# A mixer's output gates: six at the end and ten in the branch phase, or all sixteen between the stages of its heads

## The chip, the cores and the metric

The kernel runs on one core of a Trainium2 chip. The metric is the device time of one execution in microseconds (us): before the change 2744.16 us, the median of three runs (2744.15 to 2745.08).

## What is computed

The reference runs three residual blocks over 512 tokens of width 1024: twice a mixer and a gated convolutional feed-forward layer (`DEPTH = 2`), then a second kind of block with four mixers and an MLP. The change touches the mixer of the first two. Cut to what matters:

```
p = h @ w_in                                  # h: 512 x 1024, normalised
qkv, z, beta_r, a_r, hq, hf_fwd, hf_bwd, hi, hgate, gate_dn, gate_hg = split(p)
# four heads of a gated delta rule, forward and backward in time
o_dn = gated_rmsnorm(delta(q, k, v, beta, g) + flip(delta(flip(...))), z, dn_norm)
# four heads of HGRN2, forward and backward
o_hg = gated_rmsnorm(hgrn2(...) + flip(hgrn2(flip(...))), hgate, hg_norm)
merged = sigmoid(gate_dn) * (o_dn @ w_branch_dn) + sigmoid(gate_hg) * (o_hg @ w_branch_hg)
x = x + merged @ w_out
```

`gate_dn` and `gate_hg` are 1024 wide each: the sixteen output gates are the sixteen column blocks of 128 of the two. They depend on `h` alone, not on any head.

## The kernel before

Activations lie transposed, 128 features on the partitions by 512 tokens. A matrix product is a `gemm` (L264) of one block of 128 output columns: `weights` (L236) loads the weight block `wr` by a DMA of the SP queue (three buffers), ACT casts it to `wh` (L245) and DVE makes the remainder `wl` (L246), two buffers each; then three matmuls for each of the eight blocks of 128 input features (`xh wh`, `xl wh`, `xh wl`, L257 through `mm`) add up in one of two PSUM banks `pd`. So a gate is 24 matmuls, an `evac` on DVE (L394) that multiplies by the norm `rb`, and a sigmoid on ACT (L746). A branch product has four input blocks and is 12 matmuls.

`mixer` (L719) has two phases. In the **head phase** the string `ORDER` (L171) sets the stages: for each of four heads a `gdn_front` (f: three gemms, a convolution), a `gdn_inverse` (i: six levels in which PE, DVE and ACT wait for each other, L528 to L540), an `hg_head` (h: four gemms, then seven levels over the tile `pq`, L680 to L690) and a `gdn_scan` (s: four steps, each a chain of `pp`, `r`, `pw`, `w`, `pu`, `S2`, L580 to L603). Scan and `hg_head` end in `head_out` (L616): a gemm, the square of the output (L623), its sum over the partitions by a matmul with ones (L299), Ln and Exp (L294, L295), a product on POOL (L626) and one on DVE (L628). The scan loads its decays `er` by a DMA of the ACT queue (L566), takes their exponential on ACT (L567) and multiplies on POOL (L569). Each engine works its own list in order; a scheduler that lays the instructions out on a modelled timeline makes the lists, stages that come earlier in `ORDER` ahead, inverses and scans raised in priority, so that gemms of later stages stand between the links of their chains.

After the heads come six gates whose matmuls are **paced**: `mm` queues them behind marked steps of the last scan, eight after each mark (`PACE`, L259). In the **branch phase** the outputs are split into `xh` and `xl` (L286, L287); for each of eight m come a product with `w_bh` (evacuated at L764), one with `w_bd` (L768), a sum on POOL (L769), a split, and two further gates, ten in all, computed when they are next needed. Six buffers `g` hold the gates. Then `w_out`.

## Time and profile before

| | |
|---|---|
| median of three runs | 2744.16 us |
| span of the profiled execution, first to last instruction | 2742.3 us |
| median less this span | 1.9 us |
| PE busy, share of the span | 2645.3 us, 96% |
| DVE, ACT, POOL busy | 57%, 41%, 12% |
| mean granted TensorE clock | 0.983 of 2.4 GHz |

The profile is of one execution; the pages and stretches below count from its first instruction. Head phase and last scan lie at about 0 to 440 us in the first mixer and 950 to 1390 in the second, the branch phases at 440 to 540 and 1390 to 1495. PE's busy time counts matmuls whose pipelines overlap: one of 512 columns is shown with 0.39 us but the next starts 0.23 us after it, so a busy PE isn't always at its pace, and the number of matmuls in a stretch says more than its busy time. PEclk is the granted clock; 0.5 is 1.2 GHz.

### The profile page before, as it was taken

Reading aid. Unit: us, or ns where it says so; the run is one execution under the profiler, and the core shown is the slowest. Engines: PE = TensorE matmul, PEld = TensorE weight load, DVE = VectorE, ACT = ScalarE, POOL = GpSimd, SP = SyncE. Lnnn points to the kernel's source line nnn. Section 1 sums busy time; section 2 is a strip of 40 time slices with the busy share of each in tenths; the row PEclk is TensorE's granted clock in tenths of the full one; section 3 lists DMA queues with packets and bytes.
Section 4 is the critical chain, followed back from the end, with each engine's and each line's share of the span. In section 5 each row is a group of like instructions: output and inputs, shape, how many; then the busy total and the mean of one; then the engine's idle time right before and its main releaser. Section 6 shows DMA issues by size and latency. Waiting matters only on the chain.

```text
span 2742.3 us, 32455 instructions
## 1 busy us (share of the span) xinstructions
PE 2645.3 (96%) x12674; PEld 2178.6 (79%) x12674; DVE 1556.6 (57%) x2234; ACT 1124.7 (41%) x1511; POOL 329.2 (12%) x282
## 2 busy tenths in 40 slices
PE   7999899999999979998999999999999999999999
PEld 4788788878888857887888788888777788888887
DVE  6778764455554366778644555534874444553442
ACT  6545544343333255455443433333446443332221
POOL 1112320001110011122200011100100111000000
PEclk9999989999999999999999999999999999999999
DMA  4112212253223332111123423234411232433332
GB/s 149 62 49 67 62 39 68 88 167 100 94 98 114 121 89 70 55 61 54 39 76 101 160 95 100 93 121 127 145 64 51 82 96 94 140 129 99 94 104 88
DMA packets 99064, 254.13 MB, mean 93 GB/s; under 512 B 10016, under 2 KB 31520, under 8 KB 98656
## 3 DMA queue, kind: packets, MB, share of 16 engines
q1 hardware_dynamic: 66960, 215.17, 24.5%
q10 hardware_dynamic: 31568, 35.85, 4.5%
q8 instruction: 100, 1.64, 0.2%
q0 software_dynamic: 384, 1.05, 0.1%
q14 instruction: 52, 0.43, 0.1%
HBM read 238.36 MB, written 12.62 MB: 92 GB/s over the span
## 4 chain that ended last, share of the span: by engine, by line
PE 49%; ACT 1%; DVE 0%; issue 0%; POOL 0%; ACTq 0%; DVEq 0%; POOLq 0%
PE pd L257 45%; PE ph L1065 1%; PE pl L1053 1%; PE pd L259 1%; ACT wh L245 0%; PE pr L1061 0%; ACT L1179 0%; PE pl L972 0%; PE ph L682 0%; PE pl L843 0%; DVE wl L246 0%; ACT rb L294 0%; ACT rb L295 0%; PE pl L1015 0%; PE ph L1039 0%
## 5 line engine op out<-in xcount | busy, mean ns | idle before, releaser
L257 PE MATMUL pd<-xh,wh 128*128 128x512 f32 (+1 forms) x3186 | 1265.8, 398 | 36.3 <-DVE raw L449 14.3
L257 PE MATMUL pd<-xh,wl 128*128 128x512 f32 (+1 forms) x3188 | 1258.0, 395 | 2.6 <-DVE wl L246 2.3
L257 PE MATMUL pd<-xl,wh 128*128 128x512 f32 (+1 forms) x3186 | 1253.7, 394 | 2.1 <-DVE xl L290 2.0
L245 ACT ACTIVATE wh<-wr 128x1024 fp32r<-128x1024 f32 (+5 forms) x449 | 434.9, 969 | 1011.3 <-PE pd L257 866.8
L257 PEld LDWEIGHTS pd<-xh,wh 128*128 128x128 f32 (+1 forms) x3186 | 600.2, 188 | 178.8 <-issue 20.9
L257 PEld LDWEIGHTS pd<-xl,wh 128*128 128x128 f32 (+1 forms) x3186 | 600.3, 188 | 139.2 <-issue 7.2
L257 PEld LDWEIGHTS pd<-xh,wl 128*128 128x128 f32 (+1 forms) x3188 | 600.0, 188 | 138.7 <-DVE wl L246 5.0
L246 DVE TENSOR_TENSOR wl<-wr,wh 128x1024 fp32r<-128x1024 f32 (+5 forms) x449 | 521.7, 1162 | 250.3 <-ACT wh L245 244.1
L1179 ACT ACT_TABLE_LOAD x116 | 148.8, 1283 | 8.7 <-issue 4.4
L394 DVE TENSOR_TENSOR g<-pd,rb 128x512 f32<-128x512 f32 x64 | 44.3, 692 | 158.2 <-PE pd L257 148.1
L803 POOL TENSOR_TENSOR fs<-fs,rb 128x512 f32<-128x512 f32 x44 | 56.9, 1294 | 506.3 <-ACT fs L802 506.3
L682 PE MATMUL ph<-pq,kc 128*128 128x128 f32 x448 | 74.8, 313 | 19.6 <-POOL er L569 6.7
L797 DVE TENSOR_TENSOR fg<-pd,rb 128x512 f32<-128x512 f32 x44 | 30.5, 693 | 109.9 <-PE pd L257 107.0
L682 PEld LDWEIGHTS ph<-pq,kc 128*128 128x128 f32 x448 | 66.7, 213 | 26.4 <-issue 19.2
L687 POOL TENSOR_TENSOR pq<-pq,f 128x512 f32<-128x512 f32 x48 | 58.8, 1225 | 230.7 <-PE ph L682 211.5
L805 DVE TENSOR_TENSOR fs<-fs,pd 128x512 f32<-128x512 f32 x44 | 30.3, 688 | 90.0 <-POOL fs L803 90.0
L801 DVE SCALAR_TENSOR_TENSOR fs<-fg,cv,fs 128x512 f32<-128x512 f32 x88 | 65.9, 749 | 3.6 <-ACT fs L799 1.9
L802 ACT ACTIVATE fs<-fs 128x512 f32<-128x512 f32 x44 | 27.8, 632 | 85.5 <-DVE fs L801 85.5
L394 DVE TENSOR_TENSOR mh<-pd,rb 128x512 f32<-128x512 f32 x32 | 22.1, 692 | 70.2 <-PE pd L257 68.8
L680 ACT COPY kc<-qk 128x512 f32<-128x512 f32 x56 | 36.9, 659 | 52.2 <-PE ph L682 44.5
L454 DVE SCALAR_TENSOR_TENSOR qk<-raw,cv,qk 128x512 f32<-128x512 f32 x64 | 54.1, 858 | 2.6 <-ACT qk L452 2.2
L684 DVE COPY_PREDICATED att<-um,ph 128x512 f32<-128x512 uint8 x56 | 41.2, 736 | 21.5 <-PE ph L682 21.2
(332 smaller groups left out, 2442.5 us busy)
## 6 DMA issues: line engine op xcount, KB each, us to landing
wr<-in_w_in_dram SPq DMA_DIRECT2D x126, 512.0 KB, 3.3
wr<-in_w_up_dram SPq DMA_DIRECT2D x88, 512.0 KB, 3.3
wr<-in_w_m_dram SPq DMA_DIRECT2D x64, 512.0 KB, 3.8
wr<-in_w_dn_dram SPq DMA_DIRECT2D x32, 512.0 KB, 3.6
wr<-in_w_gt_dram SPq DMA_DIRECT2D x32, 512.0 KB, 3.3
wr<-in_w_out_dram SPq DMA_DIRECT2D x24, 512.0 KB, 3.4
xd<-xn ACTq DMA_DIRECT2D x40, 256.0 KB, 2.0
xo<-xd ACTq DMA_DIRECT2D x32, 256.0 KB, 2.8
```

The source lines that it names most:

```text
L245: nc.scalar.activation(hi, raw, AF.Copy)
L246: (nc.vector if lo == "v" else nc.gpsimd).tensor_tensor(lw, raw, hi.bitcast(F32), op=ALU.subtract)
L257: return self.nc.tensor.matmul(*a, **k)
L394: self.nc.vector.tensor_tensor(out, ps, rb, op=ALU.mult)
L454: V.scalar_tensor_tensor(o, raw[:, j:j + T], self.col(f"dnc{l}_{j}", ch), o, op0=ALU.mult, op1=ALU.add)
L680: A.copy(kc.rearrange("p (n e b) -> p n e b", e=2, b=hh), self.pair(qk, T, hh, 0, 0, T))
L682: PE.matmul(pl[:, c], kc[:, c * P:(c + 1) * P], self.pair(pq, T, hh, 1, c * P, P), start=True, stop=True)
L684: V.copy_predicated(att, self.um[:, o:o + P].unsqueeze(1).to_broadcast([P, 4, P]), pl)
L687: (G if hh > 1 else V).tensor_tensor(halves(pq, hh, True), halves(pq, hh, True), tot(F, n, 0, n + 1, hh), op=ALU.mult)
L801: nc.vector.scalar_tensor_tensor(g, gp[:, j:j + T], self.col(f"fc{l}_{j}", m), g, op0=ALU.mult, op1=ALU.add)
L803: nc.gpsimd.tensor_tensor(g, g, rb, op=ALU.mult)
L1179: nc.scalar.preload_act_table_set(s)
```

## The change

The six gates after the heads and the ten of the branch phase go. `ORDER` gets ten times `g1` and a last `g6`: all sixteen gates are computed in the head phase, as stages of their own. The first ten are stored unscaled to DRAM (`gs`, SP queue) and come back in the branch phase into tiles `gl` of their own (SP queue); the last six stay in the `g` buffers. All sixteen sigmoids are taken at the branch phase's start. `issue_after`, the marks and `PACE` are gone. Docstrings, which are gone as well, are left out here.

```
-NP = 6
-PACE = 8
-ORDER = "f0 i0 f1 h0 s0 i1 f2 h1 s1 i2 f3 h2 s2 i3 h3 s3"
+KEEP = 6
+NL = 10
+ORDER = "f0 i0 f1 g1 h0 g1 s0 g1 i1 f2 g1 h1 g1 s1 g1 i2 f3 g1 h2 g1 s2 g1 i3 h3 g1 s3 g6"
...
     def mm(self, *a, **k):
-        if not self.pace:
-            return self.nc.tensor.matmul(*a, **k)
-        with self.tc.issue_after(self.pace[0]):
-            self.nc.tensor.matmul(*a, **k)
-        self.paced += 1
-        if self.paced % PACE == 0:
-            self.pace.pop(0)
+        return self.nc.tensor.matmul(*a, **k)
...
+                def gate():
+                    i = len(gates)
+                    s = self.evac(self.gemm([W[(GD0, GH0)[i % 2] + i // 2]], xs), rb, gt, "g", NG)
+                    if i < 2 * KD - KEEP:
+                        t = self.dr.tile([P, T], F32, name=self.nmx("gs"), tag=f"gs{i}")
+                        nc.sync.dma_start(t, s)
+                        s = t
+                    gates.append(s)
...
+                    if u[0] == "g":
+                        for _ in range(h):
+                            gate()
...
-                for i in range(NG - NP):
-                    gate(i)
-                self.pace = self.marks[:]
-                for i in range(NG - NP, NG):
-                    gate(i)
-                self.pace = []
...
+                for i in range(2 * KD):
+                    t = gates[i] if i >= 2 * KD - KEEP else mg.tile([P, T], F32, name=self.nmx("gl"), tag="gl", bufs=NL)
+                    if i < 2 * KD - KEEP:
+                        nc.sync.dma_start(t, gates[i])
+                    nc.scalar.activation(t, t, AF.Sigmoid)
+                    gates[i] = t
...
-                        for i in range(2 * m - 2 + NG, min(2 * m + NG, 2 * KD)):
-                            gate(i)
```

What it does to the engines' lists is seen at three places of the first mixer. Numbers behind a name tell tiles apart; the changed kernel's lines are some ten lower (L254 is L257 here, L669 is L682, L520, L527 and L530 are L528, L535 and L538, L291 is L299, L278 is L286).

**PE, the last head's inverse and `hg_head`** (`pl` banks are the inverse's levels, `ph` the levels of `hg_head`). Before:

```order
L528 MATMUL pl_552_2869<-zt_529_2773,br_527_2769 128x128 x4
L682 MATMUL ph_599_3117<-pq_570_2939,kc_600_3118 128x128 x4
L535 MATMUL pl_554_2876<-v_553_2874,zc_555_2877 128x128 x4
L538 MATMUL pl_556_2883<-zc_555_2877,v_553_2874 128x128 x4
L682 MATMUL ph_601_3128<-pq_570_2939,kc_602_3129 128x128 x4
L528 MATMUL pl_557_2890<-zt_529_2773,br_527_2769 128x128 x4
L682 MATMUL ph_603_3139<-pq_570_2939,kc_604_3140 128x128 x4
L535 MATMUL pl_559_2897<-v_558_2895,zc_560_2898 128x128 x4
L538 MATMUL pl_561_2904<-zc_560_2898,v_558_2895 128x128 x4
L682 MATMUL ph_605_3150<-pq_570_2939,kc_606_3151 128x128 x4
L545 MATMUL pl_564_2913<-zt_529_2773,bn_526_2767 128x128 x4
L682 MATMUL ph_607_3161<-pq_570_2939,kc_608_3162 128x128 x4
```

In the changed list, at the same place:

```order
L254 MATMUL pd_716_3728<-xh_10_111,wh_718_3730 128x512
L254 MATMUL pd_716_3728<-xl_11_112,wh_718_3730 128x512
L254 MATMUL pd_716_3728<-xh_10_111,wl_719_3731 128x512
L669 MATMUL ph_649_3410<-pq_624_3254,kc_650_3411 128x128 x4
L254 MATMUL pd_716_3728<-xh_12_116,wh_718_3730 128x512
L254 MATMUL pd_716_3728<-xl_13_117,wh_718_3730 128x512
L254 MATMUL pd_716_3728<-xh_12_116,wl_719_3731 128x512
L254 MATMUL pd_716_3728<-xh_15_123,wh_718_3730 128x512
L254 MATMUL pd_716_3728<-xl_16_124,wh_718_3730 128x512
L527 MATMUL pl_613_3212<-v_612_3210,zc_614_3213 128x128 x4
L530 MATMUL pl_615_3219<-zc_614_3213,v_612_3210 128x128 x4
L254 MATMUL pd_716_3728<-xh_15_123,wl_719_3731 128x512
```

No gemm stood between the levels from pl_547 of the inverse to its end; now some 5 to 24 matmuls of gates (pd_716 to pd_741, the last six) stand between one level and the next. The late levels of the other heads have gates or gemms between most of them as well.

**PE, the end of the last scan.** Before, the scan's outputs (L607, L606) and its sum of squares (L299) stand among the gates pd_671, pd_676 and pd_681:

```order
L257 MATMUL pd_671_3480<-xl_31_159,wh_673_3482 128x512
L607 MATMUL pr_627_3265<-gb_418_2167,w_647_3329 128x128
L606 MATMUL pr_627_3265<-er_624_3252,s_643_3311 128x128
L607 MATMUL pr_627_3265<-gb_418_2167,w_647_3329 128x128
L257 MATMUL pd_671_3480<-xh_30_158,wl_674_3483 128x512
```

```order
L257 MATMUL pd_676_3514<-xl_31_159,wh_678_3516 128x512
L299 MATMUL pr_654_3371<-sqd_653_3369,ones_82 128x512
L257 MATMUL pd_676_3514<-xh_30_158,wl_679_3517 128x512
L257 MATMUL pd_681_3548<-xh_10_111,wh_683_3550 128x512
```

Now the last gate ends at the second of the scan's four steps (in the second mixer at the third), twelve branch matmuls stand behind it, and from there on the list has only the scan, the end of `hg_head` and the two sums of squares ahead of the first branch products pd_772 and pd_776:

```order
L700 MATMUL ph_669_3513<-pq_624_3254,hs_664_3488 128x128
L702 MATMUL ph_669_3513<-pq_624_3254,hs_664_3488 128x128
L698 MATMUL ph_669_3513<-att_646_3402,it_644_3397 128x128
L700 MATMUL ph_669_3513<-pq_624_3254,hs_664_3488 128x128
L291 MATMUL pr_714_3721<-sqd_713_3719,ones_82 128x512
L291 MATMUL pf_676_3560<-sqh_675_3558,ones_82 128x512
L254 MATMUL pd_772_4002<-xh_764_3986,wh_774_4004 128x512
L254 MATMUL pd_776_4022<-xh_764_3986,wh_778_4024 128x512
```

What was the scan's last cover has moved ahead of it, and the last `hg_head` now ends behind the scan.

**ACT, the passage to the branch phase.** Before:

```order
L295 ACTIVATE sqd_653_3369<-sqd_653_3369 128x512
L1179 ACT_TABLE_LOAD
L746 ACTIVATE g_680_3545<-g_680_3545 128x512
L286 ACTIVATE xh_694_3606<-o_492_2623 128x512
L286 ACTIVATE xh_698_3614<-o_623_3250 128x512
L286 ACTIVATE xh_700_3618<-o_655_3376 128x512
L346 DMA xo_833_4323<-in_x_dram 128x512
L346 DMA xo_849_4372<-in_x_dram 128x512
L245 ACTIVATE wh_708_3644<-wr_707_3643 128x512
L746 ACTIVATE g_685_3579<-g_685_3579 128x512
L245 ACTIVATE wh_712_3664<-wr_711_3663 128x512
L245 ACTIVATE wh_718_3689<-wr_717_3688 128x1024
```

Now:

```order
L278 ACTIVATE xh_768_3994<-o_677_3565 128x512
L278 ACTIVATE xh_770_3998<-o_715_3726 128x512
L338 DMA xo_853_4363<-in_x_dram 128x512
L338 DMA xo_869_4412<-in_x_dram 128x512
L1171 ACT_TABLE_LOAD
L750 ACTIVATE gl_746_3934<-gl_746_3934 128x512
L750 ACTIVATE gl_747_3937<-gl_747_3937 128x512
L750 ACTIVATE gl_748_3940<-gl_748_3940 128x512
L244 ACTIVATE wh_782_4044<-wr_781_4043 128x512
L750 ACTIVATE gl_749_3943<-gl_749_3943 128x512
L244 ACTIVATE wh_788_4069<-wr_787_4068 128x512
L750 ACTIVATE gl_750_3946<-gl_750_3946 128x512
```

The sigmoids of the stored gates stand ahead of the casts of the third to fifth branch weights (wh_782, wh_788, wh_792). On the SP queue the ten loads `gl` stand behind the first five branch weights and ahead of the sixth; the first of them waits for the last `hg_head`'s output (L615, o_677), whose buffers' place the tiles take. Each of the ten stores stands in the list of SP four weight loads behind the weights of its gate.

## Rows read from the trace of the kernel before

**Rows 1.** The page's first part, engines over the whole span.

```profile
PE 2645.3 (96%) x12674; PEld 2178.6 (79%) x12674; DVE 1556.6 (57%) x2234; ACT 1124.7 (41%) x1511; POOL 329.2 (12%) x282
```

**Rows 2.** Busy time by stretch: length, then busy us and number of instructions of PE, PEld, DVE, ACT and POOL, the granted clock, the DMA engines' share, GB/s. The head phases of the two mixers and stretches of them.

```profile
60.00:412.00 352.00, 324.34 (x1853) 280.48 (x1854) 267.05 (x414) 181.56 (x240) 88.82 (x66) 0.95 0.18 56
220.00:280.00 60.00, 60.00 (x371) 52.80 (x370) 45.27 (x73) 31.59 (x42) 16.12 (x12) 1.00 0.16 53
280.00:345.00 65.00, 55.82 (x314) 47.20 (x313) 55.06 (x84) 33.11 (x48) 18.30 (x15) 0.93 0.20 57
380.00:412.00 32.00, 26.01 (x145) 23.48 (x144) 24.21 (x41) 12.87 (x21) 10.69 (x9) 0.79 0.10 29
1060.00:1363.00 303.00, 281.30 (x1664) 246.25 (x1662) 226.45 (x363) 144.74 (x196) 72.22 (x55) 0.95 0.18 55
1230.00:1300.00 70.00, 59.92 (x349) 51.67 (x348) 57.86 (x90) 34.72 (x51) 20.53 (x17) 0.93 0.18 53
1333.00:1363.00 30.00, 24.25 (x137) 22.00 (x135) 23.25 (x38) 11.06 (x18) 10.70 (x9) 0.77 0.10 31
```

**Rows 3.** The same stretches for the 512-column matmuls of L257 on PE alone: length, busy us and number, clock, DMA.

```profile
60.00:412.00 352.00, 194.16 (x744) 0.95 0.18 56
220.00:280.00 60.00, 36.61 (x148) 1.00 0.16 53
280.00:345.00 65.00, 30.33 (x108) 0.93 0.20 57
380.00:412.00 32.00, 3.15 (x12) 0.79 0.10 29
1060.00:1363.00 303.00, 159.32 (x614) 0.95 0.18 55
1230.00:1300.00 70.00, 30.35 (x112) 0.93 0.18 53
1333.00:1363.00 30.00, 3.03 (x11) 0.77 0.10 31
```

**Rows 4.** The same for a stretch of the first branch phase.

```profile
470.00:560.00 90.00, 90.00 (x394) 1.00 0.33 102
```

**Rows 5.** Instructions in order of time at the end of the first mixer's first `hg_head`: start, us, engine, line, operation, tiles; in brackets how long its engine had stood idle and for whom.

```profile
206.72 0.93 ACTq L566 DMA_DIRECT2D er<-gd  x2
...
210.12 0.61 PE L538 MATMUL pl<-zc,v 128*128 128x128 f32 x4
...
212.05 0.63 ACT L567 ACTIVATE er<-er 128x512 f32<-128x512 f32 x1 [1.97 <-DMA er<-gd]
...
212.96 1.27 POOL L569 TENSOR_TENSOR er<-er,qk 128x512 f32<-128x512 f32 x1 [2.54 <-DVE egl L568]
...
214.23 0.98 PE L682 MATMUL ph<-pq,kc 128*128 128x128 f32 x3 [3.50 <-POOL er L569]
```

**Rows 6.** Groups by line over the span: tiles, shapes, number, busy us, mean ns of one, idle time before.

```profile
L394 DVE TENSOR_TENSOR g<-pd,rb 128x512 f32<-128x512 f32 x64 | 44.3, 692 | 158.2 <-PE pd L257 148.1 <-PE pd L259 10.1
L746 ACT ACTIVATE g<-g 128x512 f32<-128x512 f32 x32 | 20.2, 632 | 8.7 <-DVE g L394 8.5
L583 DVE SCALAR_TENSOR_TENSOR r<-pr,gs,vtok 128x128 f32<-128x128 f32 x48 | 14.6, 346 | 32.4 <-PE pr L580 32.0
L592 ACT ACTIVATE w<-pr 128x256 f32<-128x256 f32 x32 | 12.0, 376 | 22.3 <-PE pl L538 12.3 <-PE pr L589 10.0
L1179 ACT ACT_TABLE_LOAD x116 | 148.8, 1283 | 8.7 <-issue 4.4 <-PEq L1212 1.7 <-DVE g L394 0.7
L294 ACT ACTIVATE sqh<-pf,biasc 128x512 f32<-128x512 f32 x8 | 5.5, 688 | 14.5 <-PE pf L299 14.5
L295 ACT ACTIVATE sqh<-sqh 128x512 f32<-128x512 f32 x8 | 5.0, 629 | 0.2
L626 POOL TENSOR_TENSOR zsh<-zsh,sqh 128x512 f32<-128x512 f32 x8 | 10.3, 1290 | 62.5 <-ACT sqh L295 62.4
L628 DVE SCALAR_TENSOR_TENSOR o<-ph,cv,zsh 128x512 f32<-128x512 f32 x8 | 6.0, 749 | 3.8 <-POOL zsh L626 3.7
L286 ACT ACTIVATE xh<-o 128x512 fp32r<-128x512 f32 x16 | 8.8, 620 | 0.5 <-DVE o L628 0.5
L287 DVE TENSOR_TENSOR xl<-o,xh 128x512 fp32r<-128x512 f32 x16 | 10.0, 686 | 2.8 <-ACT xh L286 2.8
```

**Rows 7.** The same, shapes kept apart: casts and remainders of weights.

```profile
L245 ACT ACTIVATE wh<-wr 128x512 fp32r<-128x512 f32 x32 | 20.1, 629 | 78.4 <-PE pd L257 78.4
L246 DVE TENSOR_TENSOR wl<-wr,wh 128x512 fp32r<-128x512 f32 x32 | 21.9, 683 | 0.0
L246 DVE TENSOR_TENSOR wl<-wr,wh 128x1024 fp32r<-128x1024 f32 x366 | 468.9, 1281 | 204.3 <-ACT wh L245 198.1 <-DMA bs<-in_bs_dram 3.7
```

**Rows 8.** DMA: the queue of the hardware DMAs of SP (packets, MB, its share of 16 engines' span), and the issues of 256 KB loads from DRAM with their median us to landing.

```profile
q1 hardware_dynamic: 66960, 215.17, 24.5%
xo<-xd ACTq DMA_DIRECT2D x32, 256.0 KB, 2.8
```

**Rows 9.** Instructions in order of time at the second mixer's start, where PE resumes after a pause.

```profile
1015.64 0.77 PE L257 MATMUL pd<-xh,wh 128*128 128x512 f32 x1 [10.39 <-DVE raw L449]
1017.06 0.63 PE L257 MATMUL pd<-xh,wh 128*128 128x512 f32 x1
1017.49 0.63 PE L257 MATMUL pd<-xl,wh 128*128 128x512 f32 x1
```

More of the change, by code (lines that the diff above doesn't have):

```diff
@@ L187, in __init__ @@
         self.n = 0
-        self.pace, self.paced = [], 0
         self.cm = self.cp.tile([P, I["cm"].shape[1]], F32, name="cm")
@@ L572, in gdn_scan @@
             S = None
-            marks = []
             for step in range(4):
@@ L579, in gdn_scan @@
                     for d, c in enumerate(cs):
-                        i = PE.matmul(pp[:, d], kT[:, c * P:(c + 1) * P], S[:, d], start=True, stop=True)
-                    marks.append(i.ins)
+                        PE.matmul(pp[:, d], kT[:, c * P:(c + 1) * P], S[:, d], start=True, stop=True)
                     for d, c in enumerate(cs):
@@ L588, in gdn_scan @@
                 for d, c in enumerate(cs):
-                    i = PE.matmul(pw[:, d], zf[:, d, c], rs[d], start=True, stop=True)
-                marks.append(i.ins)
+                    PE.matmul(pw[:, d], zf[:, d, c], rs[d], start=True, stop=True)
                 w = gp.tile([P, 2, P], F32, name=self.nmx("w"), tag="w")
@@ L596, in gdn_scan @@
                     for d, c in enumerate(cs):
-                        i = PE.matmul(pu[:, d], kd[:, d, c], w[:, d], start=True, stop=True)
-                    marks.append(i.ins)
+                        PE.matmul(pu[:, d], kd[:, d, c], w[:, d], start=True, stop=True)
                     if S is None:
@@ L609, in gdn_scan @@
                     S = S2
-        self.marks = marks
         return self.head_out(l, h, flat(po), self.I[f"w_in{l}"][Z0 + h], f"dnn{l}", xs, rb, gp, sp, (("zsd", 1), ("sqd", 1), "pr", "od"))
@@ L740, in mixer @@
                         dn[h] = self.gdn_scan(l, h, xs, rb, sm, gp, sp, fr[h], zf[h])
-                W = self.I[f"w_in{l}"]
-                gates = []
-                def gate(i):
-                    s = self.evac(self.gemm([W[(GD0, GH0)[i % 2] + i // 2]], xs), rb, gt, "g", NG)
-                    nc.scalar.activation(s, s, AF.Sigmoid)
-                    gates.append(s)
-                for i in range(NG - NP):
-                    gate(i)
-                self.pace = self.marks[:]
-                for i in range(NG - NP, NG):
-                    gate(i)
-                self.pace = []
             with tc.tile_pool(name=f"ma{l}", bufs=1) as ma, tc.tile_pool(name=f"mg{l}", bufs=1) as mg:
```

4 lines of the change are left out of this document (3 added, 1 removed).

## Prediction

> **What bounds the kernel now.** I read the page's engine shares first: PE is busy for 96% of the span [rows 1], no other engine for more than 57%. That doesn't mean that PE is at its pace, so the second view is the number of matmuls by stretch. In the branch phase 394 matmuls of 512 columns start in 90 us [rows 4], one every 0.228 us: there PE is the bound, and no change of order gains anything. In the head phase the matmuls are mixed with smaller ones. A dense stretch of it, 220 to 280 us, has 371 matmuls, 148 of them of 512 columns [rows 2, 3]; 148 x 0.228 = 33.8 us, so the other 223 take 26.2 us, 0.1175 us each. With these two prices every stretch says how long its matmuls need at full pace; the rest of it is open time, in which PE waits or runs at half its clock.
>
> - First mixer, 60 to 412 us: 744 x 0.228 + 1109 x 0.1175 = 300.2 us needed of 352, so 51.8 us open [rows 2, 3].
> - Second mixer, 1060 to 1363 us: 614 x 0.228 + 1050 x 0.1175 = 263.6 of 303, so 39.4 us open.
> - Of these 91 us, most lie in four stretches where a head's inverse and `hg_head` end: 280 to 345 (65 - 48.9 = 16.1 us), 380 to 412 (13.6), 1230 to 1300 (16.6) and 1333 to 1363 (12.7), together 59. There the granted clock is 0.77 to 0.93 [rows 2].
>
> Two kinds of waiting make the open time. In the last head the levels follow one another with no gemm between them: the chain alone sets the pace. In the others a queue jams: at 206.72 ACT's queue issues the load of `er`, ACT stands until it lands and takes the exponential at 212.05, POOL's product follows at 212.96, the next product of `pq` behind it, and PE's next level stands idle 3.5 us for it [rows 5].
>
> **The change, part by part.**
>
> *Matmuls.* The same number. A gate is 24 x 0.228 = 5.5 us of PE. Ten gates, 55 us for each mixer, leave the branch phase, where each costs its full 5.5 us, and go to the head phase, where it costs what the open time doesn't give. So the gain is the open time that they fill. Six more move from the last scan to the last head's levels.
>
> *How much is filled.* The order shows 5 to 24 gate matmuls, 1.1 to 5.5 us, between successive levels of the last head, where a level had none; so PE and not the chain should set the pace there, and I take 80% of 26.3 us, 21 us. The stretches before have jams, which order can't remove; but where gates stand between levels the chains run ahead of PE and a 3.5 us jam meets slack. I take 60% of 32.7, 20 us. The remaining 32 us are scattered, in part the start of the first inverse with nothing ahead of it: 35%, 11 us. Together 52 us of 91 (57%). The bounds: a quarter (23 us), if jams only move, and 85% (77 us), if only the start stays open.
>
> *DVE and ACT in the head phase.* Each gate brings one remainder (1281 ns) and one evacuation (692 ns) to DVE [rows 6, 7], 20 us for ten. DVE was busy for 267 of 352 us [rows 2]; 287 us in a phase that becomes some 30 us longer is 75%, as before. It is covered on average, but not in 280 to 345 us, where DVE is at 85%; this is why I take 60% there and not 80%. The sigmoids (632 ns, [rows 6]) leave the chain of a gate and cost nothing in the head phase.
>
> *Stores.* Twenty stores of 256 KB, against a DMA share of 0.18 [rows 2]: no cost in traffic. In SP's list a store waits for an evacuation with weight loads behind it. Four weight loads stand between the gate's weights and its store, and the next load needs a buffer that is free only when that gate's matmuls are over; so the store adds at most the evacuation, 0.7 us, to a load that is needed more than one gemm later. Zero; at worst 20 x 0.7 = 14 us.
>
> *The last scan without its cover.* In the first mixer two of its steps, in the second one, have no gate beside them any more. A step keeps DVE and ACT for 4 x 346 + 376 ns = 1.8 us [rows 6], some 3 us with its hand-overs; twelve branch matmuls (2.7 us) still stand between. I take 3 us for the first mixer and 1.5 us for the second.
>
> *The passage to the branch phase.* Before, three gates and more lay under the end of the heads. Now PE has two sums of squares and then waits for the last `hg_head`. From its last matmul: square 0.6 and hand-over 0.2, table load 1.28, twice Ln and Exp (0.69 + 0.63), two products on POOL of which the second ends at 6.1 us, DVE 0.75, so the output stands at 6.9 us; then the remainder of another head and its own `xh` and `xl` [rows 6]. The first two branch products go on at about 7.7 and end, 16 matmuls later, at 11.3 us. The stored gates can only be asked for at 6.9, since their tiles take the place of that head's buffers; a 256 KB load lands after 2.8 us [rows 8], at 9.9. Behind it ACT takes a table load, three sigmoids and the cast of the third weight (0.63 each), DVE its remainder (0.68) [rows 6, 7]: the third product starts at about 13.4. PE had 5 us of work in these 13.4, so 8.4 us are lost in each mixer. The other loads (ten are 2.62 MB; the queue moves 215.17 MB in 24.5% of the span, 320 GB/s [rows 8], so 8.2 us) come one every 0.8 us, while a product takes 2.7 us and needs about one gate: covered, though casts of the fourth and fifth weights stand behind sigmoids and are only just in time. In all 4.5 + 2 x 8.4 = 21 us, and 22 with a clock that is lower at the start. Bounds: 15, if half of the passage overlaps, and 40, if the loads land as late as `er` did (5.3 us from issue to use, [rows 5]) and the casts wait for them.
>
> **The sum.** 2742.3 - 52 + 22 = 2712 us for the profiled span; the median of the runs stood 1.9 us above the span, which gives 2714 us, 1.1% faster.
>
> **A rule of the skill that speaks against it.** After a pause of 10.39 us PE started seven matmuls 0.43 us apart before they came 0.23 apart again [rows 9]: a restart cost 7 x 0.2 = 1.4 us, and in the passage it falls partly into the wait for the third weight, so the sum has 1 us for both. The Trainium skill, "TensorE: Matmul & The Clock Gate", section "HAM oscillation", says that a wait ahead of each group of matmuls lets the clock drop, so that every group starts at half rate. The trace agrees for long pauses (0.77 in 1333 to 1363 us), and by that rule the passage, with two pauses one behind the other, would run its groups at 1.2 GHz.
>
> **The rivals.**
>
> 1. *The passage runs at half clock* (the mechanism beside that rule). 18 + 12 matmuls at 0.43 in place of 0.228 us are 6 us for each mixer: 2726 us. Against it: the two pauses lie 4 us of matmuls apart. 8%.
> 2. *Nearly everything is filled.* For: the gates stand between almost all late levels, and PE's clock stays up, so that open time at half clock goes too. 85%: 2744 - 77 + 22 = 2689 us. Against: PE's list is in order, and a matmul that waits for POOL stops the gates behind it. 18%.
> 3. *The passage eats the gain*: loads as late as `er`, sigmoids ahead of the casts, 40 us for both mixers, and 45% filled (41 us): 2743 us, no change. 10%.
> 4. *Slower: the gates don't fill.* Place: the levels of `hg_head`. The open time there is a wait of ACT for `er`, passed on to DVE, POOL and PE; gates ahead of such a level only bring PE to it later if the jam isn't yet over, and they add DVE work where it is at 85%. Then each gate costs its 5.5 us in the head phase as it did before, and the passage comes on top. It decides once less than 22 of 91 us (a quarter) are filled; at 10% it is 2744 - 9 + 22 = 2757 us. Against: in the last head nothing jams and nothing stands between the levels. 14%.
>
> That the change wouldn't do what it says is excluded by the order: the gates stand between the stages.
>
> **How the numbers follow.** My case has 50%: 2714 us, itself good for 2704 to 2728 (fill 45 to 68%). The range takes in rivals 1 and 3, most of 2 and the nearer half of 4: 2690 to 2752 us, leaving out about 2 in 10. What a measurement can tell from no change is 0.2%, 5.5 us. Faster by more: 50 + 8 + 18 = 76%; the same: 10%; slower: 14%.
>
> **What would show it.** Right: in the last head's levels PE at a clock near 1.0 with matmuls of gates between them; the head phases with some 40 us open in place of 91; the branch phases some 55 us shorter; between the last `hg_head` matmul and the third branch product some 13 us with PE mostly idle, the loads `gl` landing about 3 us after that head's output; POOL and ACT named as what PE waits for. Wrong: idle PE ahead of levels with gates before them, DVE or a store on SP as releaser, weights that land late behind a store, or a passage of 20 us and more.

## The result, and the profile after

The changed kernel takes 2716.5 us (median of four runs, 2714.8 to 2720.1); the kernel before took 2744.2 beside it (2741.5 to 2745.1). The ratio is 0.9905, interval 0.9891 to 0.9919: faster by 27.6 us, about 1%. The forecast was 2714. The profiled execution has a span of 2716.0 us, 26.3 less than before; the rows below are from it.

Line numbers have moved: the gemm's matmuls are now L254 (L257 before), the sums of squares L291, casts and remainders of weights L244 and L245, those of data L278 and L279, a head's output L610 to L615, the evacuation L386, the exponential of `er` L559. First the page's engines and its row of SP's queue, beside [rows 1, 8].

```profile
PE 2635.0 (97%) x12674; PEld 2166.1 (80%) x12674; DVE 1538.2 (57%) x2234; ACT 1121.9 (41%) x1510; POOL 335.1 (12%) x282
q1 hardware_dynamic: 72720, 225.66, 25.6%
```

PE has the same 12674 matmuls and is busy 10 us less; the queue carries 10.5 MB more, the stores and loads of twenty gates. Now the stretches, with the columns of [rows 2]: the first mixer's heads up to its last scan, the 28 us of that scan, 14 us from the last `hg_head` matmul on, and the second mixer's heads up to its last scan.

```profile
60.00:452.00 392.00, 384.48 (x2166) 330.99 (x2167) 285.84 (x434) 193.82 (x252) 85.43 (x63) 0.99 0.22 73
452.00:480.00 28.00, 27.06 (x175) 23.98 (x174) 12.24 (x29) 6.63 (x13) 2.88 (x3) 1.00 0.12 36
480.00:494.00 14.00, 7.71 (x20) 4.50 (x19) 4.09 (x6) 9.73 (x15) 2.50 (x2) 0.76 0.44 144
1037.00:1402.00 365.00, 349.77 (x1987) 301.17 (x1987) 249.69 (x395) 169.28 (x222) 71.61 (x54) 0.98 0.21 69
```

And of these the 512-column matmuls of L254, beside [rows 3].

```profile
60.00:452.00 392.00, 277.40 (x1082) 0.99 0.22 73
452.00:480.00 28.00, 14.31 (x59) 1.00 0.12 36
480.00:494.00 14.00, 5.48 (x12) 0.76 0.44 144
1037.00:1402.00 365.00, 247.24 (x939) 0.98 0.21 69
```

At the prediction's prices, 0.228 us for these and 0.1175 us for the others, the first mixer's heads need 1082 x 0.228 + 1084 x 0.1175 = 374.1 of 392 us: 17.9 us are open where 51.8 were. The second's need 939 x 0.228 + 1048 x 0.1175 = 337.2 of 365: 27.8 open where 39.4 were. So 45.5 of 91 us are filled, 34 in the first mixer and 12 in the second. The last scan (175 matmuls, 59 of them of 512 columns, 27.1 of 28 us at these prices) has 0.9 us open. The 14 us behind it held 12 gemm matmuls and a few sums, at a clock of 0.76: that is the passage, shown here in order of time.

```profile
480.03 0.39 PE L700 MATMUL ph<-pq,hs 128*128 128x128 f32 x2
...
480.45 0.60 ACT L610 ACTIVATE sqh<-ph 128x512 f32<-128x512 f32 x1 [1.64 <-PE ph L700]
...
484.32 0.63 ACT L287 ACTIVATE sqh<-sqh 128x512 f32<-128x512 f32 x1
485.03 1.27 POOL L613 TENSOR_TENSOR zsh<-zsh,sqh 128x512 f32<-128x512 f32 x1
...
486.33 0.75 DVE L615 SCALAR_TENSOR_TENSOR o<-ph,cv,zsh 128x512 f32<-128x512 f32 x1 [0.49 <-POOL zsh L613]
487.12 0.63 ACT L278 ACTIVATE xh<-o 128x512 fp32r<-128x512 f32 x1 [2.17 <-DVE o L615]
...
487.16 5.50 SPq L749 DMA_DIRECT2D gl<-gs  x10
...
487.80 1.22 PE L254 MATMUL pd<-xh,wh 128*128 128x512 f32 x2 [5.57 <-ACT xh L278]
...
488.82 0.63 PE L254 MATMUL pd<-xl,wh 128*128 128x512 f32 x1
...
490.77 0.63 ACT L750 ACTIVATE gl<-gl 128x512 f32<-128x512 f32 x1 [0.69 <-DMA gl<-gs]
...
493.42 0.61 ACT L244 ACTIVATE wh<-wr 128x512 fp32r<-128x512 f32 x1
...
494.08 0.50 PE L254 MATMUL pd<-xh,wh 128*128 128x512 f32 x1 [0.81 <-ACT wh L244]
```

Read it down: the last `hg_head` matmul starts at 480.03 and ends at 480.42; then come square, Ln and Exp twice, POOL, DVE; the output stands at 487.1, 6.7 us after the matmul. PE had nothing to do for 5.57 us, then gives the twelve matmuls that are left of the first two branch products, 0.43 us apart. The loads of the gates are asked for at 487.16; ACT stands for the first three as they land (the bracket `<-DMA gl<-gs`), and the cast of the third weight, L244, comes behind their sigmoids at 493.42. PE's third product starts at 494.08, named as waiting for that cast. In the second mixer it is named as waiting for the evacuation of the first product, which multiplies by a gate whose sigmoid stood behind its load:

```profile
1439.92 0.47 PE L254 MATMUL pd<-xh,wh 128*128 128x512 f32 x1 [0.94 <-DVE gl L758]
```

The second mixer's biggest hole, in order of time:

```profile
1238.61 0.93 ACTq L558 DMA_DIRECT2D er<-gd  x2
...
1243.96 0.63 ACT L559 ACTIVATE er<-er 128x512 f32<-128x512 f32 x1 [3.78 <-DMA er<-gd]
...
1244.87 0.96 PE L520 MATMUL pl<-zt,br 128*128 128x128 f32 x4
...
1248.29 1.14 DVE L495 SCALAR_TENSOR_TENSOR gb<-gb,gs,cm 128x128 f32<-128x128 f32 x4 [3.50 <-DMA gb<-gd]
...
1250.99 0.68 DVE L441 TENSOR_TENSOR raw<-pd,rb 128x512 f32<-128x512 f32 x1
...
1251.73 0.80 PE L254 MATMUL pd<-xh,wh 128*128 128x512 f32 x1 [5.90 <-DVE raw L441]
...
1252.33 0.63 PE L254 MATMUL pd<-xl,wh 128*128 128x512 f32 x1
```

PE's levels stop at 1244.87 and it stands idle for 5.90 us, until DVE has done an evacuation (`raw`, L441). DVE had stood for 3.50 us in front of a subtraction that waited for its load of `gb`, with the evacuation behind it in its queue; ACT had stood 3.78 us for `er`. The matmuls behind it come 0.42 us apart, at half clock.

The kernel before had a hole of the same kind at the same place, and of nearly the same length:

```profile
1245.04 0.63 ACT L567 ACTIVATE er<-er 128x512 f32<-128x512 f32 x1 [3.98 <-DMA er<-gd]
...
1247.63 1.14 DVE L503 SCALAR_TENSOR_TENSOR gb<-gb,gs,cm 128x128 f32<-128x128 f32 x4 [1.75 <-DMA gb<-gd]
...
1253.88 0.80 PE L257 MATMUL pd<-xh,wh 128*128 128x512 f32 x1 [5.05 <-DVE zsh L394]
```

So the change didn't make this hole; it left it open.

To compare twelve more kernels I use one measure, worked out from every trace in the same way: the **lost time** of PE: for each matmul the time from its start to the next one's start, less what it needs at full pace (0.227 us for a gemm's matmul, 0.428 for a sum of squares, 0.867 ns a column and at least 0.056 us for others), and never less than nothing. "Heads" ends, and "passage" begins, 5 us ahead of a mixer's last head output; the passage goes to the first evacuation of the output projection, the first mixer's heads include the kernel's start, and the rest is everything else. Span less the sum is 2522 to 2527 us in all of them, so the measure accounts for the differences to some 5 us. Lost times and spans are of one profiled execution of each kernel, the medians of all its executions.

| kernel | heads 1 | passage 1 | heads 2 | passage 2 | rest | span | median |
|---|---|---|---|---|---|---|---|
| before | 83.8 | 1.9 | 81.0 | 1.9 | 47.2 | 2742.3 | 2744.2 |
| changed | 53.5 | 11.2 | 67.1 | 10.8 | 50.0 | 2716.0 | 2716.5 |
| e1 paced | 59.1 | 3.7 | 68.1 | 3.3 | 49.4 | 2705.9 | 2711.2 |
| e2 two gates held | 59.8 | 5.1 | 65.5 | 3.8 | 48.4 | 2705.1 | 2707.1 |
| e3 no stores or loads | 55.1 | 14.8 | 64.2 | 15.2 | 50.6 | 2724.1 | 2726.7 |
| e4 resident first | 54.2 | 11.0 | 66.2 | 10.8 | 50.7 | 2716.4 | 2717.4 |
| e5 `gb` late | 65.5 | 10.8 | 45.9 | 11.2 | 49.6 | 2705.8 | 2707.7 |
| e6 `er` doubled | 66.6 | 12.4 | 63.5 | 12.5 | 52.7 | 2733.2 | 2735.0 |
| e7 sigmoids early | 58.4 | 10.0 | 62.0 | 10.1 | 46.1 | 2710.8 | 2713.8 |
| e8 six gates alone | 74.0 | 9.3 | 70.9 | 9.9 | 51.8 | 2742.9 | 2746.3 |
| e9 `gb` late, mixer 2 | 55.7 | 10.9 | 60.3 | 11.1 | 52.5 | 2715.1 | 2716.7 |
| e10 e9 and e2 | 57.7 | 4.5 | 65.9 | 3.8 | 46.7 | 2701.2 | 2703.7 |
| e11 e9 and e1 | 60.9 | 4.1 | 52.9 | 2.8 | 49.3 | 2693.8 | 2697.0 |
| e12 e11 and e7 | 66.6 | 4.1 | 56.4 | 3.0 | 48.8 | 2702.5 | 2704.8 |

The change gained 30.3 + 13.9 us in the heads, gave back 9.3 + 8.9 in the passages and lost 2.8 in the rest. How far such numbers carry shows at two places. The rest, which no edit touches, lies between 46.1 and 52.7 us; and four kernels in which PE's list in the first mixer is the same (changed, e3, e4, e9) lost 53.5 to 55.7 us in its heads. So a few microseconds between two kernels aren't put down to an edit.

Where the heads gained is seen when they are cut up by stage. From 4 us ahead of the first level of the last `hg_head` to the first output product of the last scan, PE lost 14.8 us (first mixer) and 14.5 us (second) before, and loses 1.6 and 1.4 now. From there to the passage it loses 0.9 and 0.7 us more than before. All that lies earlier gained 18 us in the first mixer and some 2 in the second. So two questions follow: what the passage is made of, and why the earlier heads of the second mixer gained so little.

### The profile page after: what moved, and what is told of

It is laid out like the page before. It is cut to its first block, busy times and chain, and to the rows that moved or that the text cites. A ratio compares the mean times of both kernels' runs of the same rounds, so it can differ in the third digit from the quotient of the medians.

```text
span 2716.0 us, 32489 instructions
## 1 busy us (share of the span) xinstructions
PE 2635.0 (97%) x12674; PEld 2166.1 (80%) x12674; DVE 1538.2 (57%) x2234; ACT 1121.9 (41%) x1510; POOL 335.1 (12%) x282
## 4 chain that ended last, share of the span: by engine, by line
PE 89%; ACT 3%; DVE 2%; DMA 2%; issue 2%; POOL 1%; SPq 0%; ACTq 0%; DVEq 0%; POOLq 0%
PE pd L254 78%; PE ph L669 2%; DMA er<-gd 1%; ACT L1171 1%; PE pl L1045 1%; PE pl L530 1%; PE ph L1057 1%; PE pl L527 1%; PE pl L520 1%; PE pf L291 1%; ACT wh L244 1%; PE pl L537 1%; PE pr L579 1%; PE pr L595 0%; DVE wl L245 0%
## 5 line engine op out<-in xcount | busy, mean ns | idle before, releaser
L254 PE MATMUL pd<-xh,wh 128*128 128x512 f32 (+1 forms) x3240 | 1292.0, 399 | 44.7 <-DVE raw L441 19.0
L254 PE MATMUL pd<-xh,wl 128*128 128x512 f32 (+1 forms) x3240 | 1283.8, 397 | 0.6 <-DVE wl L245 0.5
L254 PE MATMUL pd<-xl,wh 128*128 128x512 f32 (+1 forms) x3240 | 1279.1, 395 | 1.9 <-DVE xl L282 1.8
L244 ACT ACTIVATE wh<-wr 128x1024 fp32r<-128x1024 f32 (+5 forms) x449 | 434.7, 969 | 958.3 <-PE pd L254 835.9
L254 PEld LDWEIGHTS pd<-xh,wh 128*128 128x128 f32 (+1 forms) x3240 | 611.6, 189 | 194.1 <-issue 22.9
L254 PEld LDWEIGHTS pd<-xl,wh 128*128 128x128 f32 (+1 forms) x3240 | 611.8, 189 | 140.1 <-issue 7.2
L254 PEld LDWEIGHTS pd<-xh,wl 128*128 128x128 f32 (+1 forms) x3240 | 611.1, 189 | 138.2 <-issue 5.5
L245 DVE TENSOR_TENSOR wl<-wr,wh 128x1024 fp32r<-128x1024 f32 (+5 forms) x449 | 511.7, 1140 | 253.4 <-ACT wh L244 246.9
L386 DVE TENSOR_TENSOR g<-pd,rb 128x512 f32<-128x512 f32 x64 | 44.0, 688 | 112.2 <-PE pd L254 112.2
L797 DVE TENSOR_TENSOR fs<-fs,pd 128x512 f32<-128x512 f32 x44 | 30.3, 688 | 90.0 <-POOL fs L795 90.0
L793 DVE SCALAR_TENSOR_TENSOR fs<-fg,cv,fs 128x512 f32<-128x512 f32 x88 | 65.9, 749 | 3.6 <-ACT fs L791 1.9
L669 PE MATMUL ph<-pq,kc 128*128 128x128 f32 x448 | 65.3, 286 | 0.0
L669 PEld LDWEIGHTS ph<-pq,kc 128*128 128x128 f32 x448 | 60.9, 192 | 3.1 <-issue 0.5
L794 ACT ACTIVATE fs<-fs 128x512 f32<-128x512 f32 x44 | 27.8, 632 | 85.5 <-DVE fs L793 85.5
L386 DVE TENSOR_TENSOR mh<-pd,rb 128x512 f32<-128x512 f32 x32 | 22.1, 691 | 70.2 <-PE pd L254 68.8
L525 ACT ACTIVATE zc<-z 128x512 fp32r<-128x512 f32 x48 | 30.7, 640 | 66.0 <-DVE z L532 59.4
```

The source lines that it names most:

```text
L244: nc.scalar.activation(hi, raw, AF.Copy)
L245: (nc.vector if lo == "v" else nc.gpsimd).tensor_tensor(lw, raw, hi.bitcast(F32), op=ALU.subtract)
L254: return self.nc.tensor.matmul(*a, **k)
L386: self.nc.vector.tensor_tensor(out, ps, rb, op=ALU.mult)
L525: A.activation(blk(zc), vz(z), AF.Copy)
L669: PE.matmul(pl[:, c], kc[:, c * P:(c + 1) * P], self.pair(pq, T, hh, 1, c * P, P), start=True, stop=True)
```

## The experiments

Each is the changed kernel with one edit or, from e10 on, with several; the kernel before had medians of 2742.6 to 2743.7 beside them. Line numbers in the rows are those of the run's own kernel.

**e1, the pacing put back.** The ten stored gates stay where they are; the last six are queued behind the last scan's steps again.

```diff
-... i3 h3 g1 s3 g6
+... i3 h3 g1 s3 p6      # p: eight matmuls of a gate behind each step of the last scan
```

> The ten stored gates stay between the stages; the matmuls of the last six are queued eight at a time behind the steps of the last scan, as in the kernel before. Theory (the passage to the branch phase costs 10 us of TensorE per mixer because no gate is left for it): a gate and a half stands behind the last head again, the passage's loss falls from 11 us to under 3 in each mixer, but the last heads lose the six gates as filler and their stretch before the last scan opens by 6 to 10 us in each; sum 2711 us, between 2703 and 2722. Rival (the removal of the pacing is what gained): over 2726. Rival (the pacing had nothing to do with the passage): 2716, with the same hole behind the last head.

2711.2 us, ratio 0.988 (0.9866 to 0.9895), within the range. The passage's loss falls to 3.7 and 3.3 us, a little above the 3 of the theory. The last head's levels lose 5.4 and 4.6 us more than in the changed kernel, somewhat less than the 6 to 10 of the theory; in sum the heads lose 5.6 us more in the first mixer and only 1.0 in the second, where earlier holes came out smaller. The 14 us that answer to 480:494 above, around the last head's output (here at 480.87):

```profile
474.00:488.00 14.00, 13.89 (x59) 10.63 (x58) 7.24 (x10) 11.68 (x16) 2.57 (x2) 1.00 0.43 152
```

59 matmuls and a clock of 1.00 where 20 and 0.76 stood. As the theory had it: the passage was open because no gate was left behind the last head.

**e2, two gates held back.** The last two of the sixteen are queued behind the last product of the last `hg_head`, without pacing.

```diff
-... i3 h3 g1 s3 g6
+... i3 h3 g1 s3 g4      # the other two gates behind all stages, with held set
...
-        return self.nc.tensor.matmul(*a, **k)
+        if not self.held:
+            return self.nc.tensor.matmul(*a, **k)
+        with self.tc.issue_after(self.tail):      # the last product of hg_head
+            return self.nc.tensor.matmul(*a, **k)
```

> Only the last two of the sixteen gates are held back, queued behind the last product of the last head; the other fourteen are as in the changed kernel. Theory: 48 matmuls of 0.228 us (10.9 us) lie in the passage, its loss of 10.1 us per mixer falls below 3; the last scan, which these two gates covered, opens by 2 to 6 us per mixer; sum 2706 us, between 2699 and 2714. Rival (the last scan and head are a chain of waits, and whatever is taken from them comes back as idle time): 2716, within 3. Rival (the passage is short of weights, not of matmuls: the casts of the gates' and of the branch weights queue up): no shorter than 2714, with the third product still 13 us behind the last head.

2707.1 us (0.9865, 0.985 to 0.9881), within the range. The same 14 us:

```profile
480.00:494.00 14.00, 13.21 (x53) 9.38 (x52) 6.58 (x11) 10.61 (x15) 1.52 (x2) 1.00 0.54 177
```

The passages gain 6.1 and 7.0 us and come to 5.1 and 3.8, not below 3. The last scan opens by 3.9 us in the first mixer and 2.5 in the second, as the theory had it (2 to 6): the two gates were cover there in both. In sum the heads lose 6.3 us more in the first mixer, which eats its gain, and 1.6 less in the second, where earlier holes came out smaller, as in e1.

**e3, no stores and no loads.** The ten sigmoids read the six resident gates instead.

```diff
-    nc.sync.dma_start(t, s)            # the stores
...
-    nc.sync.dma_start(t, gates[i])     # the loads
-    nc.scalar.activation(t, t, AF.Sigmoid)
+    nc.scalar.activation(t, gates[10 + i % 6], AF.Sigmoid)
```

> The ten early gates are neither stored nor loaded: in the branch phase the sigmoids read the six gates that are still there, over and over, and write the ten tiles that the loads filled; so the products use wrong gates for five output blocks, all other work is the same. Theory: the stores cost nothing, the loads hold the first and third product of the branch phase by 2 to 4 us per mixer; 2711 us, between 2708 and 2714. Rival (the round trip is free): 2716, within 1.5. Rival (the stores hold up the weight loads behind them on SP): below 2706.

2726.7 us (0.9943, 0.9931 to 0.9956): 10 us slower, which none of the three had. The heads lose 119.3 us in sum against 120.6, so the stores cost nothing that shows. The loss is in the passages, 3.6 and 4.4 us more than in the changed kernel; ACT's rows in the first:

```profile
488.85 1.15 ACT L744 ACTIVATE gl<-g 128x512 f32<-128x512 f32 x2 [0.86 <-DVE o L615]
...
489.91 4.25 ACT L744 ACTIVATE gl<-g 128x512 f32<-128x512 f32 x8
494.06 1.65 ACT L278 ACTIVATE xh<-o 128x512 fp32r<-128x512 f32 x3
...
495.62 3.21 ACT L744 ACTIVATE g<-g 128x512 f32<-128x512 f32 x6
...
498.74 1.13 ACT L244 ACTIVATE wh<-wr 128x512 fp32r<-128x512 f32 x2
```

With nothing to wait for, all ten sigmoids were queued ahead of the casts of the last head (`xh`, 494.06, where the changed kernel has 487.12), and six more ahead of the third weight's. The loads had kept them out of the way. So the price of the loads themselves was not measured; what was is that the place of ten sigmoids of 0.6 us in ACT's queue decides when PE resumes.

**e4, the resident gates used first.** The stored ten are made those of output blocks 3 to 7.

```diff
-W[(GD0, GH0)[i % 2] + i // 2]
+W[(GD0, GH0)[i % 2] + (i // 2 + 3) % KD]
+gates = gates[-KEEP:] + gates[:-KEEP]
```

> The order in which the gates are computed is turned: the ten stored ones are those of output blocks 3 to 7, the six that stay in SBUF those of blocks 0 to 2, which the branch phase uses first; the rest is as in the changed kernel. Theory: the loads have 25 us to land, the third product starts 2 to 4 us sooner in each mixer; 2711 us, between 2708 and 2714, as without loads. Rival (what holds the third product is the cast of its weight at half clock, not the gate): 2716, within 1.5.

2717.4 us (0.9903, 0.989 to 0.9917), no change, as the rival's number had it. The cast of the third weight does hold the product, but not for the clock's sake:

```profile
491.43 0.63 ACT L750 ACTIVATE gl<-gl 128x512 f32<-128x512 f32 x1 [0.64 <-DMA gl<-gs]
...
492.44 0.63 ACT L750 ACTIVATE gl<-gl 128x512 f32<-128x512 f32 x1 [0.38 <-DMA gl<-gs]
...
493.54 0.63 ACT L750 ACTIVATE gl<-gl 128x512 f32<-128x512 f32 x1 [0.48 <-DMA gl<-gs]
494.08 0.61 ACT L244 ACTIVATE wh<-wr 128x512 fp32r<-128x512 f32 x1
```

ACT still takes three sigmoids of loaded gates, each after a wait for its load, ahead of the third weight's cast, although only the sixth product needs the first of them. The cast itself follows the third sigmoid without a wait. Turning the order of use changes nothing while the queue's order stands.

**e5, the subtraction later.** DVE's subtraction from `gb` is queued behind the last multiplication of its head's front, in both mixers.

```diff
+    with self.tc.issue_after(last):               # y * 1/norm of the same head
         V.scalar_tensor_tensor(gb[:, d, c], gb[:, d, c], sm["gc"]...)
```

> Behind the changed kernel's worst hole (6.4 us at 1244.9 in the second mixer, and 3 us of half clock after it) DVE stands 3.5 us in front of a subtraction that waits for its load of gb, with the evacuation that TensorE needs queued behind it. Here that subtraction is queued on DVE behind the last step of its head's front, so that it comes when the load has long landed. Theory (the jam is DVE's wait for gb): the hole at the fourth head's front in the second mixer falls below 3 us, no wait of DVE for gb is left; 2709 us, between 2703 and 2714. Rival (the jam is ACT's wait for er, 3.8 us just before): the hole stays above 5 us, 2716 within 2. Rival (the inverses start later and their chain becomes the bound): over 2719.

2707.7 us (0.9868, 0.9854 to 0.9881), within the range. No wait of DVE for `gb` is left among the heads; the second mixer's heads lose 21.2 us less, the first's 12.0 us more. Whether the jam's end did that or the new order that came with it, this run can't tell; e9 asks.

**e6, `er` doubled and loaded in the front.**

```diff
-NG = 6; KEEP = 6; NL = 10
+NG = 4; KEEP = 4; NL = 12
+er = gp.tile([P, 2, 4, P], F32, tag="er", bufs=2)   # in gdn_front, loaded behind gb
```

> The tile er of the scans is doubled and loaded with gb in the front, two stages ahead, where the changed kernel loads it after the scan before has ended and lets ACT wait for it; the memory comes from keeping four gates resident and storing twelve. Theory (ACT's waits for er make the holes in the middle heads): ACT has no wait for er above 1 us left, the holes of 3.3 us at 229 and of 2.6 and 6.4 us in the second mixer fall to half; 2708 us, between 2701 and 2714. Rival (DVE's wait for gb is the longer one and the holes stay): 2716 within 3. Rival (two more stored gates lengthen the passage): over 2719.

2735.0 us (0.9966, 0.9953 to 0.9979). ACT still waits for `er` in the second mixer, 7.3 us in four waits, against 8.4 in five (first row, the changed kernel; total, number, longest):

```profile
ACT er L559 <- DMA er<-gd: 8.4, 5, 3.8
...
ACT er L561 <- DMA er<-gd: 7.3, 4, 2.1
```

The exponential was queued soon behind the earlier load, so the wait moved with it. The edit didn't take away what it should; the extra time is in the first mixer's heads (13 us), with 3 us in the two passages, which the third rival had. On ACT's waits it tells nothing.

**e7, the sigmoids in the head phase.**

```diff
     s = self.evac(self.gemm(...), rb, gt, "g", NG)
+    nc.scalar.activation(s, s, AF.Sigmoid)
...
-    nc.scalar.activation(t, t, AF.Sigmoid)
```

> The sigmoid of each of the sixteen gates is taken in the head phase, right after its evacuation and before its store, as the kernel before does with its gates; the branch phase has no sigmoid left. Theory: ACT gets 16 times 0.63 us and table loads of 1.28 us more among the heads' work, where its queue stands in front of TensorE's next product; the head phase loses 3 to 8 us per mixer, the passage gains 1 to 3; 2722 us, between 2715 and 2730. Rival (ACT has room, and the passage is held by the ten sigmoids): 2711, between 2708 and 2714. Rival (the place of the sigmoids costs nothing either way): 2716 within 1.5.

2713.8 us (0.9892, 0.9878 to 0.9905), 2.7 less than the changed kernel, under the 5.5 that can be told from no change. The passage loses 1.2 and 0.7 us less, the heads 4.9 more in the first mixer and 5.1 less in the second. In sum the heads come out even, and the 2.7 us are no more than the rest's 3.9, which the edit doesn't touch. My theory of a loss of 3 to 8 us in each mixer fits the first mixer alone. PE's and DVE's lists are those of the changed kernel but for a few instructions, so no new order explains the 5.1 us that the second mixer gained; why it gained stays open.

**e8, six gates alone.** Spread over the first six places and kept; the other ten in the branch phase; nothing stored, no pacing.

```diff
-ORDER = "... s1 g1 i2 f3 g1 h2 g1 s2 g1 i3 h3 g1 s3 g6"
+ORDER = "... s1 g1 i2 f3 h2 s2 i3 h3 s3"
```

> One part of the change alone: six gates, kept in SBUF, are spread over the first six of the places between the stages; no gate is stored, and the other ten are computed in the branch phase among the products as in the kernel before. Theory (a gate gains what the idle time at its place is worth): the middle heads' holes close by 12 to 16 us per mixer as in the changed kernel, the last head and the last scan, which had the six gates, open by 12 to 20, the passage stays covered by the branch phase's own gates; 2740 us, between 2730 and 2750. Rival (the gates of the branch phase are worth nothing as cover and the middle heads' holes are all that counts): 2722 or less.

2746.3 us (1.0007, 0.9998 to 1.0016): as slow as the kernel before. Against that kernel the heads lose 10 us less in each mixer. What lies ahead of the last head's inverse gained 10.7 and 8.5 us, somewhat less than the 12 to 16 of the theory; last head and last scan together changed by some 1 us, where 12 to 20 more were put. The passages lose 7.4 and 8.0 more, although ten gates are still to come:

```profile
455.50 1.22 PE L254 MATMUL pd<-xh,wh 128*128 128x512 f32 x2 [4.22 <-ACT xh L278]
...
456.52 0.63 PE L254 MATMUL pd<-xl,wh 128*128 128x512 f32 x1
...
460.63 0.47 PE L254 MATMUL pd<-xh,wh 128*128 128x512 f32 x1 [0.40 <-DVE g L750]
```

They stand behind the first three branch products in PE's queue, so PE waits for the last head's cast (4.22 us) as in the changed kernel. That refutes the part of my theory by which the branch phase's own gates cover the passage; what did before was the paced gates. The sum fell into my range because last head and last scan lost less and the passage more than I had put.

**e9, e5 in the second mixer alone.** PE's order in the first mixer is that of the changed kernel.

```diff
-    with self.tc.issue_after(last):
+    with self.tc.issue_after(last) if l else contextlib.nullcontext():
```

> The edit of e5_gblate in the second mixer alone; the first mixer's instructions stand as in the changed kernel. Theory (the second mixer's fill failed for DVE's waits for gb, and the first mixer lost in e5 only because its inverses were put back there too): the first mixer as in the changed kernel, the second 19 us shorter as in e5; 2698 us, between 2693 and 2703. Rival (e5 gained by a chance order that came from its first mixer): the second mixer's gain is under 10 us, 2707 or more.

2716.7 us (0.9904, 0.9887 to 0.992): no gain in the whole, and 6.8 us in the second mixer's heads, under the rival's 10: the rival holds. DVE's waits for `gb` are gone from the second mixer's heads (6.6 us in two waits in the changed kernel), and ACT's for `er` fell from 8.4 to 4.4 us:

```profile
DVE gb L495 <- DMA gb<-gd: 6.6, 2, 3.5
...
ACT er L561 <- DMA er<-gd: 4.4, 3, 2.1
```

The second mixer's heads lose 60.3 us, not 45.9. Four gaps of 1.9 to 2.8 us of lost time stand at 1236 to 1264 in place of the one of 6.1, with other releasers:

```profile
1234.10 0.88 DVE L635 TENSOR_SCALAR qk<-qk,lbt 128x512 f32<-128x512 f32 x2 [3.37 <-ACT qk L631]
...
1238.88 0.63 PE L529 MATMUL pl<-v,zc 128*128 128x128 f32 x4 [2.02 <-ACT qk L445]
...
1241.97 0.79 PE L255 MATMUL pd<-xh,wh 128*128 128x512 f32 x1 [2.01 <-DVE zsh L387]
...
1260.14 1.85 PE L651 MATMUL ph<-zsh,sqh 128*128 128x128 f32 x8 [1.71 <-ACT it L644]
```

**e10 and e11, e9 with e2 and with e1; e12, e11 with e7.**

> e9 with the last two gates held behind the last head as in e2_cover2. Theory (the two losses lie in different places and add up): 2698 less the 9 us of e2 is 2689 us, between 2684 and 2694. Rival (without the jam the second mixer's gates are needed in front of its last head, and what the passage gains is lost there): 2698 within 3.

> e9 with the last six gates paced behind the steps of the last scan as in e1_paced. Theory: 2698 less the 5 us of e1 (2716.5 to 2711.2) is 2693 us, between 2687 and 2698. Rival (the pacing and the later subtraction both put back the last head's chain): over 2700.

> e11 with the sigmoids taken right after the evacuations as in e7_early: the last gates paced, the second mixer's subtraction queued behind its front, no sigmoid in the branch phase. Theory (the three edits act in different places): 2697 less the 3 us of e7 is 2694 us, between 2688 and 2700. Rival (every edit makes the scheduler write another order, and the head phase's holes are drawn anew by some 10 us): 2701 or more, or under 2688.

2703.7 us (0.9857, 0.9842 to 0.9872), 2697.0 (0.9834, 0.982 to 0.9849) and 2704.8 (0.9861, 0.9844 to 0.9877). The passage is covered in all three, its loss 3 to 5 us per mixer. The heads of the second mixer lose 65.9, 52.9 and 56.4 us: the parts don't add up. e10 is 13 us faster than e9 where e2 alone gained 9, 6 of them in the rest; it misses its theory's range and its rival's, since e9 had missed. e11 is in its range by luck: it is 20 us faster than e9 where e1 alone gained 5, with another order in the second mixer. e12 is 8 us slower than e11, as its rival had the number, but not for the rival's reason: PE's and DVE's lists are those of e11 but for an instruction or two, so no other order was drawn. What differs is ten sigmoids a mixer in ACT's list among the heads, and the heads lose 5.7 and 3.5 us more, about what e7's theory had put (3 to 8). e11 beats both kernels: 45.6 us below the one before, 19.5 below the changed one.

## Why the prediction came out

The number (2714) and the sign were right. Some terms came out for their reasons, others by errors that cancelled.

- *The fill* was set at 52 of 91 us; by the same count it was 45.5. The last head's levels filled in both mixers, from 14.8 and 14.5 us of lost time to 1.6 and 1.4, some 90% where 80% were put. What failed is the step that priced the earlier stretches for both mixers alike ("where gates stand between levels the chains run ahead of PE and a 3.5 us jam meets slack"). It held in the first mixer, which gained 18 us there and filled 34 of 51.8 us in all (65%). In the second, which gained some 2 us there and filled 12 of 39.4 in all (29%), the jam of `er` and `gb` met no slack: PE stood idle for 5.90 us where it had stood 5.05.
- *Why there?* The two mixers come from the same lines. In the kernel before, the last 1669 matmuls up to the last head output stand in the same order in both; in the changed kernel, the last 46. So with gates between the stages the scheduler wrote two different orders. Twelve kernels with ten gates between the stages lost between 45.9 and 68.1 us in the second mixer's heads. Those whose list of PE there is mostly the changed kernel's (e1 to e4, e7) lost 62.0 to 68.1; those with another list (e5, e6, e9 to e12) 45.9 to 65.9. The room was there: ahead of the last `hg_head`'s levels e5 and e11 gained 23 us in the second mixer, where the changed kernel gained 2. That DVE's wait for `gb` sat in the biggest hole is shown; that it caused the shortfall is not: without it (e9) the time was the same, and other waits of in-order queues took its place. What would give the low figure on purpose stays open.
- *The jam* in [rows 5] was read by a name in a bracket that doesn't fit. PE's level at 214.23 is put down to POOL's product with `er`, but it reads `pq`, which POOL had finished at 210.42, and `kc`, which ACT copied from 213.53 to 214.13, behind the exponential of `er` and a cast; its weight load of `kc` starts at 214.20. From the kernel before:

```profile
209.12 1.30 POOL L687 TENSOR_TENSOR pq<-pq,f 128x512 f32<-128x512 f32 x1 [12.93 <-PE ph L682]
...
213.53 0.60 ACT L680 COPY kc<-qk 128x512 f32<-128x512 f32 x1
```

  So ACT's queue held PE directly, and POOL's product with `er` is no link of that chain. That ACT stood for `er` holds.
- *The passage* was priced at 8.4 us per mixer and cost 9.3 and 8.9 more than before. The output came 6.7 us after the last `hg_head` matmul (6.9 forecast), the third product 13.7 us after it (13.4). The term that was too small is PE's own work in between: sixteen branch matmuls were put, and twelve were left, 0.9 us less. Two more parts were wrong and did not show. The loads landed after a median of 5.1 us, and the first sigmoid came 3.6 us behind the first request, where 2.8 was put:

```profile
gs<-g SPq DMA_DIRECT2D x20, 256.0 KB, 2.0
gl<-gs SPq DMA_DIRECT2D x20, 256.0 KB, 5.1
```

  Against that, the third product started on the cast alone, while the sum had it wait 0.68 us more for the remainder. And the first two products ran 0.43 us apart for 11 spacings, 2.2 us per mixer where the sum had 1 for both; that cost was absorbed, since ACT came to the third weight's cast no sooner than 493.42.
  The Trainium skill, "DMA: Bandwidth & Descriptors", section "Anatomy of one DMA — SWDGE (gpsimd) path", has some 2.0 us plus the bytes over 436 GB/s for a transfer that GpSimd issues, by which I estimate 2.6 us for 256 KB. The rows above, of another path, have the stores near it and the ten loads not.
- *Rival 1*, the passage at half clock, is half seen. The granted clock was 0.76 over these 14 us. The products after the pause of 5.57 us came at 1.2 GHz; the third, after 0.81 us, came at full pace within a few matmuls. The Trainium skill, "TensorE: Matmul & The Clock Gate", section "HAM oscillation", has each group of matmuls behind a wait start at half rate. The trace agrees for the long pause; behind the short one no group started at half rate.
- *The last scan* without its cover: 3 us forecast for the first mixer, 0.9 measured. But the prediction looked at the scan alone. Before, the pacing also kept gates for the passage: PE started 48 gemm matmuls, two gates' worth, between the last output of the scan at 445.1 and the cast of that head's output at 456.9. Taking them away is what opened the passage.
- *Stores* at zero: e3's heads show no cost beyond the 2 us or so by which equal lists differ. *Sigmoids* in the head phase, where the changed kernel has none: put back there they cost 3.5 to 5.7 us a mixer in three cases and gained 5.1 in the fourth (e7, e12).
- *DVE* was 73% busy in the first mixer's heads (75% forecast).
- One slip in the sums: a fill of 45% gives 2725 us by the prediction's own terms, not the 2728 that bounds its main case.

So the whole is: 44 us gained where gates fill the heads' idle time, 18 us given back in the passage for want of a gate behind the last head, 3 us in the rest (the sum is 23, the spans differ by 26). Against the forecast, the heads filled 6 us less, the passages cost what was put (18), the last scans 3 less, and the rest, for which nothing was put, 3 more. The pacing put back gains 5.4 us; pacing with the later subtraction gains 19.5, of which the second mixer's heads gave 14 by an order that nobody chose.
